# Four order edges, and four products ahead of the bonus sums, in the token mixers of a decoder layer

## The chip, the cores and the metric

The kernel runs on one core of a Trainium2 chip. The metric is the device time of one execution in microseconds. The engines are TensorE (PE in the profile; its weight loads are PEld), VectorE (DVE), ScalarE (ACT), GpSimd (POOL) and SyncE (SP), which here only issues loads. Each engine works through its own list of instructions in the order in which it was written, and semaphores hold an instruction until what it needs is there.

## The reference

One decoder layer on 256 tokens of width 2048, all in float32. The part that matters here is the mixer: one input product `z = rms_norm(x) @ w_in` (2048 by 4384), whose columns go to a causal pooling mixer (1024 columns) and to RWKV-7 time mixing (16 heads of 64). Each RWKV part is shifted in time before use:

```python
def token_shift(z, mu):                      # zr, zk, zv and the gates
    z_prev = pad(z)[:, :-1]
    return z + (z_prev - z) * mu

def step(S, inp):                            # per head, S is 64 x 64
    r_t, w_t, k_t, v_t, a_t, b_t = inp       # a = -kk, b = kk * gate, kk = k normed per head
    sa = einsum('bhij,bhj->bhi', S, a_t)
    S = S * w_t[:, :, None, :] + sa[..., None] * b_t[:, :, None, :] + v_t[..., None] * k_t[:, :, None, :]
    return S, einsum('bhij,bhj->bhi', S, r_t)

y = group_norm(y) + sum(r * k * r_k, -1) * v   # the second term is the "bonus"
x = x + concat(pool_out, y * g) @ w_out
```

A squared-ReLU channel mixer (2048 to 8192 and back), a gated embedding input and a last RMSNorm follow. The change does not touch these.

## The kernel before

Every large product is done as three float32r products: a weight panel `raw` of 128 x 1024 is loaded, ScalarE casts it into the high part `wh` (two casts of 512, L167) and VectorE subtracts to get the low part `wl` (L168, `split_w`). TensorE then does high by high, high by low and low by high. Panels, high parts and low parts have three buffers each. `gemm_toks` is a generator of such products; a product of the input matrix has eight panels, with twelve matmuls of 512 columns for each (L241, L242, L238).

The order on TensorE is written by hand. A queue holds the generators of the input products, in the order zk0, zr0, zv0, zk1, zr1, zp0, zv1, zp1 (the digit is the head group, or the half of the pool columns). `fill(us)` takes about so many microseconds of matmuls from the head of that queue and puts them between the small products of the RWKV part, so that TensorE has work while the other engines prepare the next small product. `finish` takes a generator to its end. On VectorE, ScalarE and GpSimd a scheduler sets the order: it works with its own estimate of times and takes what it holds to be ready, by program order and by the numbers given to `tc.high_priority`. `tc.issue_after(x)` adds an edge: what is issued inside it stands behind `x` in the order.

The RWKV part is done in chunks of 64 tokens, for two groups of eight heads each, called 0 and 1:

- `z_product`: the product's banks are copied with the norm's scale (zk1s, L488), transposed back to columns on TensorE (zkT, L498) and shifted: ScalarE writes `zk_t` (L335), VectorE adds the earlier token (L336).
- `rwkv_k`: squares of the keys (tF, L585), their sums (kkn, L595), the reciprocal norm, and the operands BK and AR of the scores. `rwkv_r` adds the part with zr.
- `inverse`: the inverse of a triangular 32 x 32 block of all heads, as 31 dependent steps on VectorE. Each step is two small operations on the tile X (L724 multiplies, L728 adds); then X is transposed and copied out (L732 to L743). It is a generator too; `beside` and `pace` let it move on a step for each so many microseconds of queue work, and `run` takes it to its end.
- `rwkv_values`: products vt, whose copies go to the tiles UV (L783), and the bonus sums bsum (L523), multiplied by VectorE (L788).
- `rwkv_scores`: for each chunk c a pair of banks of products sc (L669), copied under the mask into SC by VectorE (L676).
- `rwkv_merge`, then `rwkv_core`: chunk by chunk, rym (L821, L834) is copied to R (L818), multiplied to um (L854), copied to UV (L858), multiplied to the state's increment sm (L863), which is copied or added into the state sbd (L872, L874).
- `pool_in` copies the banks of zp0 to a tile zt (L950).

The small products draw on four banks with the tag "rw", which are given out again when their reader is done. zr1's transposes, the bonus sums and the first two pairs of scores of group 1 use the same two of them, one after the other.

The change and the prediction speak of the place between the products zk1 and zv1: group 1 gets its keys and scores, while the inverse of group 0 runs beside them, and then the core of group 0 runs with the inverse of group 1 beside it.

## Time and profile before

| | |
|---|---|
| three runs | 1176.19, 1178.42, 1178.53 us (median 1178.42) |
| profiled execution | 1177.08 us, of which the span is 1175.1 |
| TensorE | 1160.5 us busy, 6407 matmuls |
| VectorE | 877.2 us busy |
| ScalarE | 713.3 us busy |
| granted TensorE clock | 0.998 |
| mixers | from 0 to about 330 us of the span |

The rows of the prediction come from several views of one profiled execution. The page gives the busy time of each engine and the chain of work that ended last. The list of waits gives, for an instruction's line, whom it waited for, the sum, the count and the longest. Rows of the timeline give start, time, engine, line, operation, the tile written and the tiles read (buffer numbers left out), sizes, the count of instructions that were merged, and in brackets the engine's idle time ahead of it and what ended it. The view by windows gives the busy time of each engine inside a stretch. A row's time holds the way through the engine, so the next instruction of an engine often starts before the row's end; how fast an engine goes on is read from the starts.

### The profile page before, as it was taken

Reading aid. Unit: us, or ns where it says so; the run is one execution under the profiler, and the core shown is the slowest. Engines: PE = TensorE matmul, PEld = TensorE weight load, DVE = VectorE, ACT = ScalarE, POOL = GpSimd, SP = SyncE. Lnnn points to the kernel's source line nnn. Section 1 sums busy time; section 2 is a strip of 40 time slices with the busy share of each in tenths; the row PEclk is TensorE's granted clock in tenths of the full one; section 3 lists DMA queues with packets and bytes.
Section 4 is the critical chain, followed back from the end, with each engine's and each line's share of the span. In section 5 each row is a group of like instructions: output and inputs, shape, how many; then the busy total and the mean of one; then the engine's idle time right before and its main releaser. Section 6 shows DMA issues by size and latency. Waiting matters only on the chain.

```text
span 1175.1 us, 17401 instructions
## 1 busy us (share of the span) xinstructions
PE 1160.5 (99%) x6407; PEld 971.5 (83%) x6407; DVE 877.2 (75%) x1194; ACT 713.3 (61%) x1323; POOL 57.2 (5%) x133
## 2 busy tenths in 40 slices
PE   9999999999999999999999999999999999999997
PEld 8788777888888888888888888888888888888886
DVE  8686996964656666766998997676768988897543
ACT  8776858676545565555664664555556665677543
POOL 2100000000000000000110110000000110000000
PEclk9999999999999999999999999999999999999999
DMA  8464443354465555565686787555555886975511
GB/s 293 155 202 145 138 137 120 120 180 153 169 199 172 185 181 197 191 220 181 204 254 222 220 253 223 188 190 191 185 193 171 253 253 220 320 245 190 197 55 72
DMA packets 67253, 224.42 MB, mean 191 GB/s; under 512 B 7712, under 2 KB 8480, under 8 KB 66784
## 3 DMA queue, kind: packets, MB, share of 16 engines
q1 hardware_dynamic: 60240, 207.38, 51.6%
q0 software_dynamic: 6496, 15.21, 5.7%
q8 instruction: 50, 0.82, 0.3%
q10 hardware_dynamic: 432, 0.73, 0.2%
q14 instruction: 35, 0.29, 0.1%
HBM read 221.19 MB, written 2.10 MB: 190 GB/s over the span
## 4 chain that ended last, share of the span: by engine, by line
PE 95%; DVE 2%; ACT 1%; issue 0%; DMA 0%; POOL 0%; SPq 0%; DVEq 0%; POOLq 0%
PE u_w L1112 20%; PE u_w L1117 10%; PE d_b L1270 7%; PE d_b L1269 7%; PE d_b L1271 7%; PE d_w L1270 2%; PE d_w L1269 2%; PE d_w L1271 2%; PE gt_b L241 2%; PE gt_b L242 2%; PE gt_b L238 2%; PE zk_b L241 1%; PE zk_b L242 1%; PE o_b L238 1%; PE o_b L241 1%; PE o_b L242 1%
## 5 line engine op out<-in xcount | busy, mean ns | idle before, releaser
L1112 PE MATMUL u_w<-h,wh_u 128*128 128x512 f32 x1024 | 321.9, 396 | 0.0
L167 ACT ACTIVATE wh_u<-raw_u 128x512 fp32r<-128x512 f32 x256 | 147.6, 624 | 162.5 <-issue 100.9
L168 DVE TENSOR_TENSOR wl_u<-raw_u,wh_u 128x1024 fp32r<-128x1024 f32 x128 | 156.6, 1224 | 105.0 <-ACT wh_u L167 103.5
L1117 PEld LDWEIGHTS u_w<-h,wl_u 128*128 128x128 f32 x1024 | 192.5, 188 | 45.3
L1117 PE MATMUL u_w<-h,wl_u 128*128 128x256 f32 x1024 | 201.2, 278 | 0.0
L1112 PEld LDWEIGHTS u_w<-h,wh_u 128*128 128x128 f32 x1024 | 156.0, 189 | 0.2
L168 DVE TENSOR_TENSOR wl_gt<-raw_gt,wh_gt 128x1024 fp32r<-128x1024 f32 x24 | 29.4, 1224 | 23.3 <-ACT wh_gt L167 23.1
L172 ACT ACTIVATE wad<-ring 128x512 fp32r<-128x512 f32 x29 | 18.2, 628 | 44.2 <-DVE ring L1320 44.2
L167 ACT ACTIVATE wh_gt<-raw_gt 128x512 fp32r<-128x512 f32 x48 | 27.9, 635 | 24.3 <-PE gt_b L242 17.1
L241 PE MATMUL gt_b<-wh_gt,h 128*128 128x512 f32 x96 | 37.5, 390 | 0.0
L242 PE MATMUL gt_b<-wh_gt,h 128*128 128x512 f32 x96 | 37.4, 390 | 0.0
L1322 DVE TENSOR_TENSOR raw_d<-raw_d,ring 128x1024 f32<-128x1024 f32 x29 | 35.5, 1223 | 0.7
L1239 POOL DMA_DIRECT2D ring<-in_w_ffn_down_dram x29 | 16.5, 568 | 355.8 <-DVE wad L173 355.2
L1240 POOL DMA_DIRECT2D ring<-in_w_ffn_down_dram x29 | 25.4, 874 | 110.9 <-DMA ring<-in_w_ffn_down_dram 110.9
L168 DVE TENSOR_TENSOR wl_o<-raw_o,wh_o 128x1024 fp32r<-128x1024 f32 x16 | 19.6, 1222 | 12.9 <-ACT wh_o L167 9.9
L167 ACT ACTIVATE wh_o<-raw_o 128x512 fp32r<-128x512 f32 x32 | 18.4, 623 | 16.3 <-issue 8.5
L167 ACT ACTIVATE wh_zp<-raw_zp 128x512 fp32r<-128x512 f32 x32 | 18.6, 623 | 15.7 <-PE zp_b L242 7.2
L168 DVE TENSOR_TENSOR wl_zk<-raw_zk,wh_zk 128x1024 fp32r<-128x1024 f32 x16 | 19.4, 1220 | 9.1 <-ACT wh_zk L167 9.1
L241 PE MATMUL zv_b<-wh_zv,hTh 128*128 128x512 f32 x64 | 26.0, 406 | 0.0
L238 PE MATMUL gt_b<-wl_gt,h 128*128 128x512 f32 x96 | 25.8, 389 | 0.0
L241 PE MATMUL zp_b<-wh_zp,hTh 128*128 128x512 f32 x64 | 25.7, 401 | 0.0
L168 DVE TENSOR_TENSOR wl_zv<-raw_zv,wh_zv 128x1024 fp32r<-128x1024 f32 x16 | 19.4, 1218 | 8.2 <-ACT wh_zv L167 7.3
(927 smaller groups left out, 3012.4 us busy)
## 6 DMA issues: line engine op xcount, KB each, us to landing
raw_u<-in_w_ffn_up_dram SPq DMA_DIRECT2D x128, 512.0 KB, 4.2
raw_d<-in_w_ffn_down_dram SPq DMA_DIRECT2D x99, 512.0 KB, 4.9
ring<-in_w_ffn_down_dram POOLq DMA_DIRECT2D x58, 256.0 KB, 5.0
raw_gt<-in_w_ple_gate_dram SPq DMA_DIRECT2D x24, 512.0 KB, 4.1
raw_zk<-in_w_in_dram SPq DMA_DIRECT2D x16, 512.0 KB, 3.8
raw_zr<-in_w_in_dram SPq DMA_DIRECT2D x16, 512.0 KB, 3.3
raw_zv<-in_w_in_dram SPq DMA_DIRECT2D x16, 512.0 KB, 3.3
raw_zp<-in_w_in_dram SPq DMA_DIRECT2D x16, 512.0 KB, 3.2
```

The costliest lines, as they stand in the source:

```text
L167: nc.scalar.activation(wh[:, a * 512 : (a + 1) * 512], raw[:, a * 512 : (a + 1) * 512], AF.Copy)
L168: nc.vector.tensor_tensor(wl, raw, wh.bitcast(F32), op=ALU.subtract)
L238: nc.tensor.matmul(banks[tt], ah[:, ts_], halves[a][1], start=False, stop=last)
L241: nc.tensor.matmul(banks[tt], ah[:, ts_], halves[a][0], start=i + a == 0, stop=False)
L242: nc.tensor.matmul(banks[tt], al[:, ts_], halves[a][0], start=False, stop=False)
L1112: nc.tensor.matmul(bank[:, ct, :].rearrange("p (s t) -> p s t", s=2), wh[:, cs[ct]], hl, start=k == 0, stop=False, skip_group_check=True,)
L1117: nc.tensor.matmul(bank[:, ct, 0:T], wl[:, cs[ct]], hl[:, 0, :], start=False, stop=k == 15, skip_group_check=True)
L1240: nc.gpsimd.dma_start(slot(n), w_down[pair, hf * 16 + kp, 0, :, 1, :], accum_op=ALU.add)
L1269: nc.tensor.matmul(banks[n], ah, wh, start=first, stop=False)
L1270: nc.tensor.matmul(banks[n], ah, wl, start=False, stop=False)
L1271: nc.tensor.matmul(banks[n], al, wh, start=False, stop=last)
L1322: nc.vector.tensor_tensor(t43, t43, t2.unsqueeze(1).to_broadcast([128, 2, 512]), op=ALU.subtract)
```

## The change

Nothing that is computed changes, and no instruction is added. Four edges are added, most of them through a table `behind`, and one fill:

- the casts of panel zr1_2 stand behind the second copy zk1s;
- step 17 of the inverse of group 0 stands behind the last key shift of group 1, and the generator waits for that shift to have been written down;
- the casts of panel zv1_2 stand behind the copies R of the first chunk of group 0;
- the copies zt of the first pool product stand behind the first UV copy of the core (`started`); before, they were made when that product ended;
- `rwkv_values` takes 0.90 us of queue work (four low-part matmuls of zp0) between the vt products and the bonus sums for group 0, and the fill ahead of group 1's scores is cut from 8.39 to 7.47 for it.

```diff
--- before.py
+++ after.py
@@ -158,13 +158,14 @@
         nc.sync.dma_start(raw[:, 0:n], src)
         return raw
 
-    def split_w(raw, name):
+    def split_w(raw, name, after=None):
 
         wh = wp.tile([128, 1024], F32R, tag="wh", name=f"wh_{name}")
         wl = wp.tile([128, 1024], F32R, tag="wl", name=f"wl_{name}")
         with tc.high_priority(20000):
             for a in range(2):
-                nc.scalar.activation(wh[:, a * 512 : (a + 1) * 512], raw[:, a * 512 : (a + 1) * 512], AF.Copy)
+                with tc.issue_after(after.ins) if after is not None else ExitStack():
+                    nc.scalar.activation(wh[:, a * 512 : (a + 1) * 512], raw[:, a * 512 : (a + 1) * 512], AF.Copy)
             nc.vector.tensor_tensor(wl, raw, wh.bitcast(F32), op=ALU.subtract)
         return [(t_h, t_l) for t_h, t_l in zip((wh[:, 0:512], wh[:, 512:1024]), (wl[:, 0:512], wl[:, 512:1024]))]
 
@@ -216,6 +217,8 @@
                             yield 0.24
         consume(banks)
 
+    behind = {}
+
     def gemm_toks(src, acts, name, consume, kps=None, hooks=()):
 
         banks = [mm_bank(f"{name}_b{i}") for i in range(2)]
@@ -225,7 +228,7 @@
             if kp in hooks:
                 hooks[kp]()
             raw = load_raw(src[kp].rearrange("p a n -> p (a n)"), 1024, f"{name}_{kp}")
-            halves = split_w(raw, f"{name}_{kp}")
+            halves = split_w(raw, f"{name}_{kp}", behind.get(f"{name}_{kp}"))
             for part in range(2):
                 for a in range(2):
                     k = kp * 2 + a
@@ -333,7 +336,7 @@
 
     def shift_evac(dst, src, mu_ap, omu_ap):
         nc.scalar.activation(dst, src, AF.Copy, scale=omu_ap)
-        nc.vector.scalar_tensor_tensor(
+        return nc.vector.scalar_tensor_tensor(
             dst[:, 1:T], src[:, 0 : T - 1], mu_ap, dst[:, 1:T], op0=ALU.mult, op1=ALU.add
         )
 
@@ -485,7 +488,9 @@
                 zt = rp.tile([128, 2, 512], F32, tag=stage, name=f"{tag}{gi}s")
             with tc.high_priority(30000):
                 for tt in range(2):
-                    nc.scalar.activation(zt[:, tt], banks[tt], AF.Copy, scale=rs1[:, tt : tt + 1])
+                    copied = nc.scalar.activation(zt[:, tt], banks[tt], AF.Copy, scale=rs1[:, tt : tt + 1])
+            if (tag, gi) == ("zk", 1):
+                behind["zr1_2"] = copied
             box.append(zt)
 
         def turn():
@@ -499,7 +504,9 @@
             for p in range(4):
                 c = PARAM_COLS[mu_name] - m0 + 4 * gi + p
                 with tc.high_priority(30000):
-                    shift_evac(dst[:, p, :], banks[p // 2][:, p % 2 * T : (p % 2 + 1) * T], col(mu_name, 4 * gi + p), omu[:, c : c + 1])
+                    shifted = shift_evac(dst[:, p, :], banks[p // 2][:, p % 2 * T : (p % 2 + 1) * T], col(mu_name, 4 * gi + p), omu[:, c : c + 1])
+            if (tag, gi) == ("zk", 1):
+                behind["key"] = shifted
             return dst
 
         gen = queued(gemm_toks(w_in[i + gi], hT, f"{tag}{gi}", consume))
@@ -721,10 +728,13 @@
         for k in range(31):
             n, m = k // 2 + 1, 31 - k
             t_ = X.rearrange("u j t -> u (j t)")[:, 512 : 512 + n * m].rearrange("u (j t) -> u j t", t=m)
-            nc.vector.tensor_tensor(
-                t_, W[:, 0:n, k : k + 1].to_broadcast([128, n, m]),
-                AT[:, k, k + 1 : 32].unsqueeze(1).to_broadcast([128, n, m]), op=ALU.mult,
-            )
+            while gi == 0 and k == 17 and "key" not in behind:
+                yield
+            with tc.issue_after(behind["key"].ins) if gi == 0 and k == 17 else ExitStack():
+                nc.vector.tensor_tensor(
+                    t_, W[:, 0:n, k : k + 1].to_broadcast([128, n, m]),
+                    AT[:, k, k + 1 : 32].unsqueeze(1).to_broadcast([128, n, m]), op=ALU.mult,
+                )
             nc.vector.tensor_tensor(W[:, 0:n, k + 1 : 32], W[:, 0:n, k + 1 : 32], t_, op=ALU.add)
             yield
         T1G = rp.tile([96, 32, 32], F32, tag=tags[0], name=f"T1G{gi}")
@@ -781,6 +791,7 @@
             for i in range(2):
                 with tc.high_priority(30000):
                     nc.scalar.activation(flat3(UV[2 * tt + i])[64:128], b[i * 64 : (i + 1) * 64, :], AF.Copy)
+        fill(0.00 if gi else 0.90)
         bon = st["rk"]
         bf, vf = flat(bon), flat(zv)
         block_sum(
@@ -791,7 +802,7 @@
         )
         st["UV"] = UV
 
-    def rwkv_core(gi, st):
+    def rwkv_core(gi, st, started=None):
         AR, pc, SC, BKt, UV = st["AR"], st["pc"], st["SC"], st["BKt"], st["UV"]
 
         YT = yb(gi, 1)
@@ -815,7 +826,8 @@
             d = flat3(dst).rearrange("s (q r x) -> s q r x", q=2, r=2)
             v = b.rearrange("s (q r x) -> s q r x", q=2, r=2)
             for r in range(2):
-                nc.scalar.activation(d[:, :, r], v[half(2 * r, y), :, r], AF.Copy)
+                copied = nc.scalar.activation(d[:, :, r], v[half(2 * r, y), :, r], AF.Copy)
+            return copied
 
         def direct(b, c, h):
             nc.tensor.matmul(
@@ -837,7 +849,9 @@
                     )
             R = Rs[:, c % 2]
             with tc.high_priority(30000):
-                two_halves(R, b, False)
+                copied = two_halves(R, b, False)
+            if (gi, c) == (0, 0):
+                behind["zv1_2"] = copied
             if 0 < c < 3:
                 for e in range(2):
                     r = slice(e * 64, e * 64 + 64)
@@ -855,7 +869,10 @@
                 if c < 3:
                     direct(b_next, c + 1, h)
             with tc.high_priority(30000):
-                nc.scalar.activation(flat3(UV[c])[0:64], ub[0:64, :], AF.Copy)
+                copied = nc.scalar.activation(flat3(UV[c])[0:64], ub[0:64, :], AF.Copy)
+            if c == 0 and started is not None:
+                with tc.issue_after(copied.ins):
+                    started()
             fill(0.72 if gi else 0.86)
             if c < 3:
                 for h in range(8):
@@ -1007,7 +1024,7 @@
     z_zk1 = z_product(4, "zk", "mu_k", 1)
     z_zr1 = z_product(2, "zr", "mu_r", 1)
     pool = []
-    p_zp0 = queued(gemm_toks(w_in[0], hT, "zp0", lambda banks: pool.append(pool_in(0, banks))))
+    p_zp0 = queued(gemm_toks(w_in[0], hT, "zp0", pool.append))
     z_zv1 = z_product(6, "zv", "mu_v", 1, "zr")
     p_zp1 = queued(gemm_toks(w_in[1], hT, "zp1", lambda banks: pool.append(pool_in(1, banks))))
 
@@ -1034,13 +1051,17 @@
     beside.clear()
     rwkv_values(0, st0, zv0)
     make_bands()
-    fill(8.39)
+    fill(7.47)
     rwkv_scores(1, st1)
     fill(0.00)
     rwkv_merge(0, st0)
     beside += [inverse(1, st1), 0.50, 0.0]
     fill(3.06)
-    core0 = rwkv_core(0, st0)
+
+    def first_pool():
+        pool[0] = pool_in(0, pool[0])
+
+    core0 = rwkv_core(0, st0, first_pool)
     mg0 = a8(0, "mg0", F32R)
     rwkv_out(0, *rwkv_norm1(0, *core0), mg0)
     rwkv_sources(1, st1)
```

On TensorE one thing moves: `bsum` stands behind four `zp_b` matmuls of L238 instead of ahead of them. The lists of GpSimd and of the loads stay as they are. On VectorE and ScalarE the scheduler makes of the edges more than they say. Three places matter.

VectorE, up to the end of the key shifts of group 1 (wl_zr1_* are subtracts, X0 the inverse of group 0, zk_t the key shifts). Before, behind the subtract of panel zr1_1 and the operations of 126 and 130 elements that now follow the shifts:

```order
L168 TENSOR_TENSOR wl_zr1_2_1412<-raw_zr1_2_1409,wh_zr1_2_1411 128x1024
L724 TENSOR_TENSOR X0_1131<-X0_1131,AT0_1130 128x120
L728 TENSOR_TENSOR X0_1131<-X0_1131 128x10x12
L724 TENSOR_TENSOR X0_1131<-X0_1131,AT0_1130 128x121
L336 SCALAR_TENSOR_TENSOR zk_t_1349<-zkT0_1350,par_sb_77,zk_t_1349 128x255
L728 TENSOR_TENSOR X0_1131<-X0_1131 128x11x11
L336 SCALAR_TENSOR_TENSOR zk_t_1349<-zkT1_1351,par_sb_77,zk_t_1349 128x255
L724 TENSOR_TENSOR X0_1131<-X0_1131,AT0_1130 128x110
L728 TENSOR_TENSOR X0_1131<-X0_1131 128x11x10
L336 SCALAR_TENSOR_TENSOR zk_t_1349<-zkT0_1350,par_sb_77,zk_t_1349 128x255
L724 TENSOR_TENSOR X0_1131<-X0_1131,AT0_1130 128x108
L336 SCALAR_TENSOR_TENSOR zk_t_1349<-zkT1_1351,par_sb_77,zk_t_1349 128x255
```

Now:

```order
L169 TENSOR_TENSOR wl_zr1_1_1389<-raw_zr1_1_1386,wh_zr1_1_1388 128x1024
L169 TENSOR_TENSOR wl_zr1_2_1412<-raw_zr1_2_1409,wh_zr1_2_1411 128x1024
L339 SCALAR_TENSOR_TENSOR zk_t_1349<-zkT0_1350,par_sb_77,zk_t_1349 128x255
L339 SCALAR_TENSOR_TENSOR zk_t_1349<-zkT1_1351,par_sb_77,zk_t_1349 128x255
L169 TENSOR_TENSOR wl_zr1_3_1446<-raw_zr1_3_1443,wh_zr1_3_1445 128x1024
L339 SCALAR_TENSOR_TENSOR zk_t_1349<-zkT0_1350,par_sb_77,zk_t_1349 128x255
L339 SCALAR_TENSOR_TENSOR zk_t_1349<-zkT1_1351,par_sb_77,zk_t_1349 128x255
L734 TENSOR_TENSOR X0_1131<-X0_1131,AT0_1130 128x126
L738 TENSOR_TENSOR X0_1131<-X0_1131 128x9x14
L734 TENSOR_TENSOR X0_1131<-X0_1131,AT0_1130 128x130
L738 TENSOR_TENSOR X0_1131<-X0_1131 128x10x13
L734 TENSOR_TENSOR X0_1131<-X0_1131,AT0_1130 128x120
```

The shifts stand ahead of eleven inverse operations that were ahead of the last of them; the subtract wl_zr1_3, which stood behind, comes between them.

VectorE, the end of the inverse of group 0 and the first copies of the scores of group 1 (T1G0 and the STREAM_TRANSPOSE rows finish the inverse; SC1 are the score copies). Before:

```order
L732 STREAM_TRANSPOSE T1G0_1646<-X0_1131 32x16x32
L168 TENSOR_TENSOR wl_zp0_4_1778<-raw_zp0_4_1775,wh_zp0_4_1777 128x1024
L732 STREAM_TRANSPOSE T1G0_1646<-X0_1131 32x16x32
L735 COPY tmp0_1132<-X0_1131 64x16x32 x2
L739 STREAM_TRANSPOSE X0_1131<-tmp0_1132 64x16x32
L168 TENSOR_TENSOR wl_zp0_5_1809<-raw_zp0_5_1806,wh_zp0_5_1808 128x1024
L739 STREAM_TRANSPOSE X0_1131<-tmp0_1132 64x16x32
L676 TENSOR_TENSOR SC1_1759<-sc0_1760,cmask_93 128x2x4x64
L676 TENSOR_TENSOR SC1_1759<-sc1_1761,cmask_93 128x2x4x64
L168 TENSOR_TENSOR wl_zp0_6_1840<-raw_zp0_6_1837,wh_zp0_6_1839 128x1024
L676 TENSOR_TENSOR SC1_1759<-sc0_1791,cmask_93 128x2x4x64
L676 TENSOR_TENSOR SC1_1759<-sc1_1792,cmask_93 128x2x4x64
```

Now:

```order
L734 TENSOR_TENSOR X0_1131<-X0_1131,AT0_1130 128x30
L738 TENSOR_TENSOR X0_1131<-X0_1131 128x15x2
L734 TENSOR_TENSOR X0_1131<-X0_1131,AT0_1130 128x16
L738 TENSOR_TENSOR X0_1131<-X0_1131 128x16
L742 STREAM_TRANSPOSE T1G0_1646<-X0_1131 32x16x32 x2
L745 COPY tmp0_1132<-X0_1131 64x16x32 x2
L169 TENSOR_TENSOR wl_zp0_6_1840<-raw_zp0_6_1837,wh_zp0_6_1839 128x1024
L749 STREAM_TRANSPOSE X0_1131<-tmp0_1132 64x16x32 x2
L683 TENSOR_TENSOR SC1_1759<-sc0_1760,cmask_93 128x2x4x64
L683 TENSOR_TENSOR SC1_1759<-sc1_1761,cmask_93 128x2x4x64
L683 TENSOR_TENSOR SC1_1759<-sc0_1791,cmask_93 128x2x4x64
L683 TENSOR_TENSOR SC1_1759<-sc1_1792,cmask_93 128x2x4x64
```

All of the inverse still stands ahead of the first score copies; the subtract wl_zp0_6, which stood behind them, stands ahead of them too.

ScalarE, from the last merge copies into SC0 on (zt0 the pool copies, R0, UV0_0 and sbd1 the core of group 0, tmp1 the start of the inverse of group 1). Before:

```order
L764 ACTIVATE SC0_950<-qm_1900 32x8x32 x4
L950 ACTIVATE zt0_1942<-zp0_b0_1584,rs_n1_175 128x512
L950 ACTIVATE zt0_1942<-zp0_b1_1585,rs_n1_175 128x512
L167 ACTIVATE wh_zv1_2_2073<-raw_zv1_2_2071 128x512
L818 ACTIVATE R0_1966<-rym_1971 64x2x128 x2
L167 ACTIVATE wh_zv1_2_2073<-raw_zv1_2_2071 128x512
L167 ACTIVATE wh_zv1_3_2149<-raw_zv1_3_2147 128x512 x2
L710 ACTIVATE tmp1_1927<-tmp1_1927 64x1024
L858 ACTIVATE UV0_0_1655<-um_1991 64x512
L872 ACTIVATE sbd1_96<-sm_1992 64x4x64 x2
L818 ACTIVATE ys0_1967<-rym_1971 64x2x128
L719 ACTIVATE tmp1_1927<-SC1_1759 32x1024
```

Now:

```order
L774 ACTIVATE SC0_950<-qm_1900 32x8x32 x4
L717 ACTIVATE tmp1_1927<-tmp1_1927 64x1024
L829 ACTIVATE R0_1963<-rym_1968 64x2x128 x2
L168 ACTIVATE wh_zv1_2_2073<-raw_zv1_2_2071 128x512 x2
L168 ACTIVATE wh_zv1_3_2149<-raw_zv1_3_2147 128x512 x2
L726 ACTIVATE tmp1_1927<-SC1_1759 32x1024
L872 ACTIVATE UV0_0_1655<-um_1988 64x512
L967 ACTIVATE zt0_2008<-zp0_b0_1584,rs_n1_175 128x512
L967 ACTIVATE zt0_2008<-zp0_b1_1585,rs_n1_175 128x512
L889 ACTIVATE sbd1_96<-sm_1989 64x4x64 x2
L829 ACTIVATE ys0_1964<-rym_1968 64x2x128 x2
```

The pool copies go behind UV0_0, the copy inside tmp1 goes ahead of R0, and the second tmp1 copy ahead of UV0_0.

## The prediction

> **What bounds the kernel now.** I read the page first, then the waits of TensorE, then the rows of TensorE, VectorE and ScalarE in order of time around each wait.
>
> ```profile
> span 1175.1 us, 17401 instructions
> PE 1160.5 (99%) x6407; PEld 971.5 (83%) x6407; DVE 877.2 (75%) x1194; ACT 713.3 (61%) x1323; POOL 57.2 (5%) x133
> ...
> PE 95%; DVE 2%; ACT 1%; issue 0%; DMA 0%; POOL 0%; SPq 0%; DVEq 0%; POOLq 0%
> ```
>
> TensorE is the bound, and 95% of the chain that ended last lies on it. A change of order can only win back the time in which TensorE waits. The waits of TensorE between 100 and 262 us are four:
>
> ```profile
> PE bsum L523 <- DVE zr_t L336: 1.0, 1, 1.0
> PE sm L863 <- ACT UV L858: 0.9, 1, 0.9
> PE zkT L498 <- ACT zk1s L488: 0.8, 2, 0.5
> PE um L854 <- ACT R L818: 0.4, 1, 0.4
> ```
>
> These are idle times. A matmul's row is longer than the 0.23 us in which the next one starts, so a little more is hidden; the starts show it (start, time, then the group):
>
> ```profile
> 127.06 0.39 PE L242 MATMUL zr_b<-wh_zr,hTl 128*128 128x512 f32 x1
> 127.98 0.33 PE L498 MATMUL zkT<-ident,zk1s 128*128 128x128 f32 x1 [0.53 <-ACT zk1s L488]
> 128.56 0.98 PE L498 MATMUL zkT<-ident,zk1s 128*128 128x128 f32 x7 [0.25 <-ACT zk1s L488]
> 129.30 0.48 PE L241 MATMUL zr_b<-wh_zr,hTh 128*128 128x512 f32 x1
> ...
> 134.02 2.16 PE L595 MATMUL kkn<-tF_t,jhead 128*32 128x256 f32 x8
> 136.11 0.50 PE L241 MATMUL zr_b<-wh_zr,hTh 128*128 128x512 f32 x1
> ...
> 156.07 1.95 PE L780 MATMUL vt<-cen,zv_t 128*128 128x128 f32 x16
> 159.01 1.96 PE L523 MATMUL bsum<-ybuf,jsum 128*128 128x512 f32 x4 [0.99 <-DVE zr_t L336]
> ...
> 173.03 0.39 PE L238 MATMUL zp_b<-wl_zp,hTh 128*128 128x512 f32 x1
> 173.35 1.26 PE L669 MATMUL sc<-AR,BK 64*128 64x128 f32 x16
> ```
>
> The change works on all of these but the last pair, which I come to below: the second group of scores starts at 173.35, only 0.1 later than the end of the matmul in front of it allows. That row decides my forecast.
>
> **The change part by part: what TensorE wins first.** ScalarE's rows there:
>
> ```profile
> 125.18 2.18 ACT L167 ACTIVATE wh_zr<-raw_zr 128x512 fp32r<-128x512 f32 x4
> 127.26 1.24 ACT L488 ACTIVATE zk1s<-zk_b,rs_n 128x512 f32<-128x512 f32 x2
> ...
> 134.20 1.31 ACT L585 ACTIVATE tF_t<-zk_t,par_sb 128x256 f32<-128x256 f32 x3 [0.23 <-DVE zk_t L336]
> ```
>
> The edge behind the key copies puts two of the four casts (0.52 each) after zk1s, so zk1s runs from 126.2 to 127.5. TensorE comes to the transposes at 127.29, and only the second of them still waits, for some 0.2. I count 1.0 won of the 1.2 between 127.29 and 128.56.
>
> The key shifts then pass eleven operations of the inverse on VectorE (each of its steps is two, L724 and L728). Walked through the new order they end at 132.9 (the last one now starts at 134.26, below). But on ScalarE half a cast (0.52) stands between the second and the third of the four squares tF (0.4 each), so the last square ends near 134.4, where 134.20 + 1.31 = 135.5 is its end now. The norm products kkn, which go one by one behind the squares, therefore end 1.1 earlier. This contains the 1.0; it does not add to it. Another 0.2 goes at the next products, which wait for the split of the reciprocal.
>
> The bonus sums bsum reuse the banks of the zr transposes and wait for VectorE's shifts of them. Four products, 4 x 0.23 = 0.9, now fill that wait, and the shifts come 2 us earlier because fewer inverse operations stand ahead of them. The wait of 159.01 - 157.86 = 1.15 goes (157.86: the sixteenth vt start of 0.11 each after 156.07). TensorE's total lead at this point is 1.1 + 0.2 + 1.15 = 2.4 us.
>
> **Where the lead ends.** The operations that were passed have not gone: they stand behind, on VectorE.
>
> ```profile
> core 0: us, PE busy (x) PEld busy (x) DVE busy (x) ACT busy (x) POOL busy (x), PEclk, DMA share, GB/s
> 129.07:173.40 44.33, 43.19 (x213) 33.52 (x211) 43.37 (x78) 25.94 (x48) 1.86 (x5) 1.00 0.45 151
> ```
>
> Between the first moved operation and the end of the first score copies VectorE is busy 43.37 of 44.33 us. It has no room to catch up in.
>
> ```profile
> 129.07 0.28 DVE L724 TENSOR_TENSOR X<-X,AT 128x126 f32<-128x126 f32 x1
> 129.39 0.29 DVE L728 TENSOR_TENSOR X<-X 128x126 f32<-128x126 f32 x1
> ...
> 132.02 0.29 DVE L724 TENSOR_TENSOR X<-X,AT 128x121 f32<-128x121 f32 x1
> 132.22 0.47 DVE L336 SCALAR_TENSOR_TENSOR zk_t<-zkT,par_sb,zk_t 128x255 f32<-128x255 f32 x1
> ...
> 134.26 0.47 DVE L336 SCALAR_TENSOR_TENSOR zk_t<-zkT,par_sb,zk_t 128x255 f32<-128x255 f32 x1
> ...
> 172.17 1.23 DVE L676 TENSOR_TENSOR SC<-sc,cmask 128x512 f32<-128x512 f32 x2
> 173.34 1.20 DVE L168 TENSOR_TENSOR wl_zp<-raw_zp,wh_zp 128x1024 fp32r<-128x1024 f32 x1
> 174.55 1.29 DVE L676 TENSOR_TENSOR SC<-sc,cmask 128x512 f32<-128x512 f32 x2
> ```
>
> The score copies stand behind the whole inverse of the first head group, before and after. The second group of score products (173.35) uses the two banks that the first copies (172.17 to 173.4) free; it starts as they end. In the new order everything that stood ahead of these copies still does, and one subtract more: wl_zp0_6, which is the row at 173.34 now. So the copies end later by three terms:
>
> - the subtract, 174.55 - 173.34 = 1.2;
> - new waits of VectorE, by my walk 0.4 at wl_zr1_4 (its cast is the one that stands between the squares), 0.3 at the split of the reciprocal (two casts now stand ahead of it), 0.3 at the first zr shift, which VectorE reaches before ScalarE has written it, and 0.2 at wl_zp0_3, whose buffer the four moved products free: 1.2. Of the 0.96 idle now I take half for waits and half for gaps between operations: 0.7 net;
> - an inverse operation right behind another starts 0.32 later (129.07, 129.39), other work starts 0.20 later (132.02, 132.22). Nineteen such pairs stand in the new stretch and sixteen in the old: 3 x 0.12 = 0.4.
>
> That is 2.3: the second scores start at 175.65 instead of 173.35. TensorE arrives there at 173.26 - 2.4 = 170.8 and waits 4.8 us. **The whole lead is lost and 2.3 us more.** Bounds: 0.2 (1.2 less all 0.96 of idle, no new wait) and 3.4 (every new wait, none of the old ones gone). I take the middle, which is where the walk ends.
>
> [...]
>
> **The core's copies and the late adds.**
>
> ```profile
> 190.33 1.27 ACT L950 ACTIVATE zt<-zp_b,rs_n 128x512 f32<-128x512 f32 x2
> 192.01 0.77 ACT L818 ACTIVATE R<-rym 64x256 f32<-64x256 f32 x2
> 194.36 1.06 ACT L710 ACTIVATE tmp<-tmp 64x1024 f32<-64x1024 f32 x1
> 195.45 0.59 ACT L858 ACTIVATE UV<-um 64x512 f32<-64x512 f32 x1
> 198.04 1.05 ACT L719 ACTIVATE tmp<-SC 32x1024 f32<-32x1024 f32 x1
> ...
> 193.33 2.36 DVE L168 TENSOR_TENSOR wl_zv<-raw_zv,wh_zv 128x1024 fp32r<-128x1024 f32 x2 [7.34 <-ACT wh_zv L167]
> 205.51 0.86 DVE L874 TENSOR_TENSOR sbd<-sbd,sm 64x256 f32<-64x256 f32 x2
> ...
> 206.73 0.39 PE L834 MATMUL rym<-sbd,AR 128*128 128x128 f32 x2
> ```
>
> All of this is counted from the end of the scores and moves with it. The panel copies zt (1.2) leave the place ahead of R, and the L710 copy takes it, so R ends 0.65 earlier, which covers most of the um wait. But ahead of UV there would stand 1.07 (L710), 0.65 (R), 4 x 0.52 (casts) and 1.06 (L719, moved up): 4.86 after 190.33, that is 195.2 instead of 195.45. The wait for um has become a longer wait for sm; the gain is 0.25. Bounds: 1.9 won if the casts yield, 0.5 lost if ScalarE comes later.
>
> The second inverse starts earlier (its transposed tile is ready at 191.4, where VectorE sat idle until 193.33), and the scheduler uses that to put nine more inverse operations, 9 x 0.31 = 2.8, ahead of the state add of 205.51. It starts 1.9 earlier and has 2.8 more to do: the add ends at 207.3 and not at 206.4. TensorE wants it at 206.73 - 0.25 = 206.5 and waits 0.8, so 0.55 is lost against now. Bounds 0 and 0.9.
>
> **The sum.** 2.3 - 0.25 + 0.55 = 2.6 us. The profiled execution took 1177.08 (span 1175.1 and 2.0 around it), which makes 1179.7. It lies 1.3 under the median of the three runs, 1178.42, so for a median I add the 2.6 to that: **1181.0 us**. Nothing after 260 us changes its order, and TensorE's own work is the same.
>
> **The rivals.**
>
> *Faster: the lead survives.* If VectorE reached the first score copies by 170.8, TensorE would keep 2.4, and 0.25 in the core: 1178.4 - 2.65 = 1175.8. For it: the four waits are real, and each edit lies on one. Against it: VectorE would have to do in under 42 us what takes 43.4 now, with one subtract more. It decides from the point where VectorE is 5 us sooner through this stretch than I walk. Chance 0.2.
>
> *No change.* VectorE finds room for the subtract in its own 0.96 of idle time, or the inverse's pairs go at 0.20 like single operations (19 x 0.12 = 2.3 less). The second scores then start 0 to 0.2 later than now, the core's 0.25 cancels that, and the late add is left or not: 1178.4 to 1178.9. For it: each new wait is under 0.5 us, and I walked them by hand. Chance 0.27.
>
> *Slower still.* The third scores need a bank that ScalarE frees with the L783 copies, which stand behind the two L743 copies and so behind the end of the inverse. I have them done 1.3 before TensorE comes. If the inverse ends 2 us later than I walk, its lateness passes to this wait as well: 1178.4 + 4.6 = 1183.0. Chance 0.08. The forecast keeps 0.45.
>
> **How the numbers follow.** A measurement of this kernel tells about 0.2%, 2.4 us, from no change. The forecast's 2.6 lies just over that; I give it 0.38 beyond and 0.07 inside. With the last rival, slower has 0.46; faster has 0.19 of its 0.2; the rest, 0.35, is no change. The range reaches from the fast rival, 1175.6, to the slow one, 1183.2; the forecast's own range is 1179 to 1182.5.
>
> **What would show it.** Right: the list of TensorE's waits no longer has bsum or zkT above 0.3, and has a new one, the score products waiting 4 to 5 us for VectorE near 171 to 176; VectorE has no idle time over 0.5 from 129 until then; sm still waits for UV, more than 1 us; a rym wait on the state add near 209. Wrong: no wait of TensorE at the scores, or the first score copies ending before 174. If that wait is under 2 us, the term of VectorE is mis-sized and the kernel is not slower.

## The result and the profile after

The changed kernel takes 1184.18 us (median of six, 1182.72 to 1185.0), the kernel before, beside it, 1177.87 (1176.19 to 1179.46). The ratio is 1.0054, with a 95% interval of 1.0044 to 1.0064: slower by 6.3 us, 5.2 to 7.5. The direction is the forecast's; the size, 2.6, is not. Of all executions behind the numbers below, one is left out: 2342 us in an experiment (e6), which nothing else repeats.

The page's own lines, after:

```profile
span 1183.0 us, 17400 instructions
PE 1163.5 (98%) x6407; PEld 973.6 (82%) x6407; DVE 878.3 (74%) x1194; ACT 713.0 (60%) x1323; POOL 57.3 (5%) x133
...
PE 90%; DVE 6%; ACT 1%; DMA 1%; issue 1%; SPq 0%; DVEq 0%; ACTq 0%
```

VectorE has 6% of the chain where it had 2%. TensorE's list of waits (total, times, longest; the changed kernel's lines stand 3 to 21 lower in the file: the score products are L676 now, the score copies L683, the weight products L241, L244 and L245):

```profile
PE sc L676 <- DVE SC L683: 4.6, 1, 4.6
PE wagT L467 <- ACT wagS L462: 1.9, 1, 1.9
PE sm L880 <- ACT UV L872: 1.4, 1, 1.4
...
PE rym L846 <- DVE sbd L891: 0.7, 1, 0.7
...
PE yt L930 <- DVE ys L924: 0.3, 1, 0.3
```

Three of the four old waits between 100 and 262 us are gone (bsum, zkT, um). One of 4.6 us has come, beside two short ones (rym, yt): the second group of score products waits for VectorE's score copies. VectorE's rows there, with the subtract wl_zp0_6 in front of the first copies, which started at 172.17 before:

```profile
173.55 1.23 DVE L169 TENSOR_TENSOR wl_zp<-raw_zp,wh_zp 128x1024 fp32r<-128x1024 f32 x1
174.70 2.06 DVE L749 STREAM_TRANSPOSE X<-tmp 64x512 f32<-64x512 f32 x2
176.67 1.23 DVE L683 TENSOR_TENSOR SC<-sc,cmask 128x512 f32<-128x512 f32 x2
```

What the prediction had not counted stands right behind that wait. TensorE's rows in order of time:

```profile
172.44 0.39 PE L241 MATMUL zp_b<-wl_zp,hTh 128*128 128x512 f32 x1
177.46 2.64 PE L676 MATMUL sc<-AR,BK 64*128 64x128 f32 x16 [4.62 <-DVE SC L683]
180.03 1.65 PE L241 MATMUL zp_b<-wl_zp,hTh 128*128 128x512 f32 x3
181.47 0.63 PE L244 MATMUL zp_b<-wh_zp,hTh 128*128 128x512 f32 x1
```

The sixteen score products take 2.64 us; before they took 1.26 (the row at 173.35 in the prediction). The next matmuls are slow as well: 0.43 from start to start at 181.47, where it is 0.23 at full speed. The view by stretches says why, in the column behind POOL: PEclk, the share of its clock that TensorE was granted.

```profile
168.46:171.88 3.42, 3.42 (x27) 2.70 (x26) 3.17 (x10) 2.32 (x6) 0.00 (x0) 1.00 0.50 169
171.88:175.29 3.41, 0.95 (x5) 0.45 (x3) 3.35 (x5) 1.15 (x2) 0.00 (x0) 1.00 0.00 0
175.29:178.70 3.41, 1.24 (x8) 1.18 (x10) 2.62 (x4) 1.83 (x2) 0.00 (x0) 0.50 0.46 154
178.70:182.12 3.42, 3.42 (x17) 2.81 (x16) 1.64 (x3) 2.85 (x7) 0.00 (x0) 0.50 0.00 0
182.12:185.53 3.41, 3.41 (x26) 2.62 (x26) 1.26 (x2) 1.71 (x5) 0.00 (x0) 1.00 0.42 151
```

From 175.29 to 182.12 the clock is at half. TensorE works in the last 4.66 us of that (from 177.46) and does half as much: 4.66 / 2 = 2.3 us are lost behind the wait.

**The whole difference between the two profiled executions**, 1184.91 - 1177.08 = 7.8 us, read from the start of the same matmul in both:

| stretch | what | us |
|---|---|---|
| to 60 us | longer wagT wait and a half clock behind it, in a part that the change leaves as it was | +2.39 |
| 125 to 171 | TensorE's lead: less waiting at zkT, kkn, the next products, bsum | -2.98 |
| 172 to 177 | the wait at the second scores | +4.70 |
| 177 to 184 | half clock | +2.34 |
| 186 to 205 | um and sm together | -0.06 |
| 213 | rym, late state add | +1.04 |
| 214 to 245 | yt and around it | +0.55 |
| behind 600 | several small ones | -0.18 |

The first row is no work of the change: such a stretch comes and goes in other programs too (last section). Without it, it is 5.4 us.

### The profile page after: what moved, and what is told of

Same layout as the page of the kernel before. It is cut to its first block, busy times and chain, and to the rows that moved or that the text cites. A ratio compares the mean times of both kernels' runs of the same rounds, so it can differ in the third digit from the quotient of the medians.

```text
span 1183.0 us, 17400 instructions
## 1 busy us (share of the span) xinstructions
PE 1163.5 (98%) x6407; PEld 973.6 (82%) x6407; DVE 878.3 (74%) x1194; ACT 713.0 (60%) x1323; POOL 57.3 (5%) x133
## 4 chain that ended last, share of the span: by engine, by line
PE 90%; DVE 6%; ACT 1%; DMA 1%; issue 1%; SPq 0%; DVEq 0%; ACTq 0%
PE u_w L1133 20%; PE u_w L1138 10%; PE d_b L1291 7%; PE d_b L1292 7%; PE d_b L1290 7%; PE d_w L1290 2%; PE d_w L1291 2%; PE d_w L1292 2%; PE gt_b L244 2%; PE gt_b L245 2%; PE gt_b L241 2%; PE zr_b L244 1%; PE zr_b L241 1%; PE o_b L244 1%; PE o_b L241 1%; PE zr_b L245 1%
## 5 line engine op out<-in xcount | busy, mean ns | idle before, releaser
L244 PE MATMUL gt_b<-wh_gt,h 128*128 128x512 f32 x96 | 37.4, 390 | 0.0
L245 PE MATMUL gt_b<-wh_gt,h 128*128 128x512 f32 x96 | 37.4, 389 | 0.0
L244 PE MATMUL zp_b<-wh_zp,hTh 128*128 128x512 f32 x64 | 26.3, 411 | 0.0
L244 PE MATMUL zk_b<-wh_zk,hTh 128*128 128x512 f32 x64 | 25.9, 405 | 0.3 <-ACT wh_zk L168 0.3
L244 PE MATMUL zv_b<-wh_zv,hTh 128*128 128x512 f32 x64 | 26.0, 406 | 0.0
L241 PE MATMUL gt_b<-wl_gt,h 128*128 128x512 f32 x96 | 25.8, 389 | 0.0
```

The source lines that it names most:

```text
L241: nc.tensor.matmul(banks[tt], ah[:, ts_], halves[a][1], start=False, stop=last)
L244: nc.tensor.matmul(banks[tt], ah[:, ts_], halves[a][0], start=i + a == 0, stop=False)
L245: nc.tensor.matmul(banks[tt], al[:, ts_], halves[a][0], start=False, stop=False)
```

## The experiments

Ratios are to the kernel before, timed beside each run. Microseconds are the ratio's distance from 1 times 1177.5.

**Without the inverse edge.** The `while` and the `issue_after` at step 17 are removed; every other edit stays.

```diff
-            while gi == 0 and k == 17 and "key" not in behind:
-                yield
-            with tc.issue_after(behind["key"].ins) if gi == 0 and k == 17 else ExitStack():
...
```

> The changed kernel without the edge that holds step 17 of the first inverse behind the key shifts; every other edit stays. Theory (the loss is made by VectorE reaching the score copies late, because of the moved inverse operations, and by TensorE's half clock after the long wait): VectorE does before the score copies what it did in the kernel before, so the second group of score products starts within 0.7 us of its old distance from the start of the first zr product of group 1; TensorE, ahead by about 2, waits there 1.5 to 3 us, and its granted clock falls for at most 1 us. Time within 1.5 us of before (1176.5 to 1179.5). Rival (the edges on ScalarE and the moved panel copies make the loss): still 3 us or more over before, 1181 or later.

1.0028 (1.0016 to 1.0039): +3.3 us. The wait at the scores and its half clock are gone as the theory expected (sc 0.4), but the time is the rival's. Rows of its waits:

```profile
PE kkn L602 <- ACT tF_t L592: 2.7, 2, 1.7
PE sm L877 <- ACT UV L869: 2.3, 2, 1.4
...
PE rym L843 <- DVE sbd L888: 0.7, 1, 0.7
...
PE sc L676 <- DVE SC L683: 0.4, 1, 0.4
```

The key shifts come behind ten inverse operations and a subtract (133.58 on VectorE; 132.63 in the changed kernel, whose head ran 2.1 us later), and a second subtract stands between the first two shifts and the last two. The casts that ScalarE does behind zk1s feed these subtracts. So the squares are late and kkn waits 2.7, which neither side expected. That the edge on these casts does it is read from the order of the rows; no run takes that edge out alone. At 162 us the lead over the kernel before is 0.2, counted from 60 us on, where the changed kernel has 3.0. With no lead left, the rest is loss: 1.0 up to the second scores, 1.2 at the late state add, 0.5 around yt, 1.1 behind 246 us, where sm of the second group waits 0.9; 0.6 comes back behind 600 us.

**The inverse edge alone**, on the kernel before.

```diff
+            if (tag, gi) == ("zk", 1):
+                behind["key"] = shifted
...
+            while gi == 0 and k == 17 and "key" not in behind:
+                yield
+            with tc.issue_after(behind["key"].ins) if gi == 0 and k == 17 else ExitStack():
```

> The kernel before with only the edge that holds step 17 of the first inverse behind the key shifts. Theory: the score copies end 1.5 to 2.5 us later than before, TensorE is about 1 to 2 us earlier there and waits 3 to 5 us, and the granted clock then stands at 0.50 for some 4 us: time over before by 3.5 to 6.5 us (1181.5 to 1184.5), most of the loss of the changed kernel. Rival (the other edges): within 1.2 us of before.

1.0044 (1.0032 to 1.0056): +5.2 us, as the theory said. From its list of waits:

```profile
PE sc L673 <- DVE SC L680: 3.6, 2, 3.2
```

and by stretches, with the clock behind the POOL column:

```profile
170.31:173.72 3.41, 1.06 (x5) 0.45 (x3) 3.38 (x5) 1.15 (x2) 0.00 (x0) 1.00 0.10 20
173.72:177.13 3.41, 2.16 (x15) 1.97 (x16) 1.57 (x3) 2.71 (x4) 0.00 (x0) 0.50 0.34 133
177.13:180.55 3.42, 3.42 (x9) 2.65 (x10) 2.05 (x3) 1.97 (x5) 0.00 (x0) 0.50 0.00 0
180.55:183.96 3.41, 3.41 (x27) 2.61 (x26) 1.21 (x2) 2.32 (x6) 0.00 (x0) 1.00 0.47 156
```

One edge is enough for the late copies (the second of them starts 1.6 later than before, counted from 60 us on), the wait and the half clock.

**What a wait costs, made on purpose.** In the kernel before, products are moved from in front of the second scores to behind them, so that TensorE comes 4.7 (e3) or 2.6 us (e4) too early. The edit of e3; e4 has 5.20 in place of 7.29 and leaves the 8.39 as it is:

```diff
-                fill(2.60 if gi else 4.55)
+                fill((0.00, 7.29, 2.60)[c - 1] if gi else 4.55)
...
-    fill(8.39)
+    fill(6.30)
```

> The kernel before with 4.7 us of weight products taken from in front of the second group of score products (2.1 of them from in front of the first) and put behind it, in front of the third; nothing else is edited. TensorE then reaches the second group 4.7 us early and waits about 4.8 us for the copies of the first; from the third group on its order is the old one. Theory (a wait of this length also halves the clock afterwards): over before by 4.7 + 2 to 3, that is 6.5 to 8 us (1184.5 to 1186), with a granted clock of 0.50 in about 4 us behind the wait. Rival (a wait costs its own length): over before by 4.2 to 5.2 us, clock 1.00 right behind the wait.

1.0059 (1.0047 to 1.0071): +6.9 us. In its list of waits:

```profile
PE sc L669 <- DVE SC L676: 4.3, 1, 4.3
```

Counted from start to start the wait is 4.53, and TensorE is 6.2 later behind the scores.

> The same with 2.6 us of products moved from in front of the second group to in front of the third: TensorE waits about 2.7 us. Theory, if the clock falls only after a wait longer than this: over before by 2.3 to 3 us, clock 1.00 behind the wait. If the clock falls after any wait in proportion: over before by 4 us or more. Rival (the products only have to be done somewhere, and the wait is hidden): within 1 us of before.

1.0035 (1.0023 to 1.0048): +4.1 us, for a wait of 2.3 in the list, 2.56 from start to start:

```profile
PE sc L669 <- DVE SC L676: 2.3, 1, 2.3
```

The stretches of the smaller one:

```profile
170.04:173.45 3.41, 1.10 (x12) 0.91 (x14) 2.74 (x4) 1.71 (x2) 0.00 (x0) 1.00 0.41 154
173.45:176.86 3.41, 3.41 (x14) 2.70 (x13) 2.11 (x3) 3.34 (x9) 0.00 (x0) 0.50 0.00 0
176.86:180.27 3.41, 3.41 (x16) 2.78 (x16) 1.18 (x2) 1.95 (x5) 0.00 (x0) 1.00 0.47 154
```

Both waits bring one stretch of 3.41 us at half clock, 1.7 us of loss, whatever their length. The wait of 2.56 costs about 1.7 times its length. That the clock needs a longer wait, as one expectation had it, is wrong.

**The wait filled with work that is worth nothing**: products of the identity with zeros, added into the panel's open bank. e5 has ten of them, e9 five.

```diff
+            if gi and c == 1:
+                for _ in range(10):
+                    nc.tensor.matmul(behind["zp0"][0], ident, sbd[0].rearrange("p a t -> p (a t)"), start=False, stop=False)
```

> The changed kernel with ten products of the identity with a tile of zeros (128x512 fp32, some 0.45 us each) in front of the second group of scores of head group 1, added into the open bank of the panel: TensorE has work in the 4.8 us in which it waits, and nothing ends earlier by it. Theory (behind the wait the loss is the half clock, because TensorE was idle): the second scores start where they start in the changed kernel, the granted clock behind them is 1.00, and the time is 2 to 2.4 us below the changed kernel: over before by 3 to 4.5 us instead of 6.3. Rival (the rows behind the wait are slow by the new order of the other engines, or by the score copies): clock 0.50 as before, over before by 5.5 to 7.5 us.

1.0064 (1.0052 to 1.0076): +7.5 us, the rival's number, but not for its reason. A product took 0.87 us and not 0.45, so ten ran 3.9 us past the wait. Behind it, and from 50 us on to the last microseconds, the clock was 1.00. Five fit:

> e5 with five products of zeros instead of ten. Ten took 8.7 us (0.87 each, not 0.45), 3.9 longer than the wait; five take 4.35 and fit into it. Theory (half clock after an idle TensorE): the second scores start within 0.6 us of their place in the changed kernel, the granted clock behind them is 1.00, no stretch of 0.50 between 50 us and 1100 us, and the time is 2 to 2.5 us below the changed kernel: over before by 3 to 4.6 us. Rival (the loss behind the wait has another cause): over before by 5.5 us or more.

1.0034 (1.0022 to 1.0047): +4.0 us against 6.3. TensorE's rows (the trace has two matmuls for each of the five products):

```profile
170.78 4.45 PE L675 MATMUL zp_b<-sbd,ident 128*128 128x512 f32 x10
175.66 1.73 PE L679 MATMUL sc<-AR,BK 64*128 64x128 f32 x16 [0.42 <-DVE SC L686]
```

and the stretch around them:

```profile
169.00:186.00 17.00, 16.44 (x111) 11.34 (x111) 12.39 (x16) 9.29 (x19) 0.00 (x0) 1.00 0.27 94
```

The second scores start no sooner, 4.88 us after TensorE has got there; only the idling is gone. With it go the half clock and 2.3 us: the two intervals (2.6 to 5.5 and 5.2 to 7.5) still overlap a little, but 2.3 is what the table has for the half clock, and from 60 us on this profile is 2.4 shorter than the changed kernel's. So the loss behind the wait is the half clock, and its cause is that TensorE had nothing to do.

**The wait filled with products of the queue.**

```diff
-                fill(2.60 if gi else 4.55)
+                fill((7.20 if c == 1 else 2.60) if gi else 4.55)
```

> The changed kernel with 4.6 us more of weight products in front of the second group of scores (7.2 instead of 2.6); the products come from the same queue, so all later ones stand 4.6 us earlier in it. Theory: the wait of 4.8 us becomes work (below 0.5 us is left), no half clock follows, and what is taken from the queue is missing at its end only: 7 us below the changed kernel, that is from 2 us under to 0.7 us over before. Rival (the products that stand ahead of later waits are what covers them): the waits of the core grow by 2 us or more in all, and the time stays 2 us or more over before.

1.0047 (1.0034 to 1.0061): +5.5 us. That is the rival's side: the products that went are missing later. At the second scores 1.3 us of waiting are left and the half clock is gone. But between gm and qm, the two steps of `rwkv_merge`, the changed kernel has twenty products for the second group; here the queue runs dry after four:

```profile
261.20 1.21 PE L241 MATMUL zp_b<-wl_zp,hTh 128*128 128x512 f32 x4
263.79 0.32 PE L767 MATMUL qm<-SC,T1G 32*64 32x64 f32 x2 [1.38 <-ACT T1G L774]
```

and a little later, by stretches:

```profile
266.11:269.52 3.41, 3.41 (x16) 3.07 (x15) 0.00 (x0) 2.77 (x7) 0.00 (x0) 0.50 0.53 209
```

TensorE waits for qm, and behind that wait the clock is at half again.

**Five subtracts to GpSimd**, in the changed kernel and in the one before, to give VectorE room.

```diff
-            nc.vector.tensor_tensor(wl, raw, wh.bitcast(F32), op=ALU.subtract)
+            (nc.gpsimd if name in ('zp0_1', 'zp0_2', 'zp0_4', 'zp0_5', 'zp0_6') else nc.vector).tensor_tensor(wl, raw, wh.bitcast(F32), op=ALU.subtract)
```

> The changed kernel with the five subtracts wl_zp0_1, 2, 4, 5 and 6 (1.2 us each on VectorE, in front of the first score copies) done by GpSimd. Theory (VectorE's work in front of the score copies is what ends TensorE's lead): the first score copies end 5 to 6 us earlier than in the changed kernel, the wait at the second scores is below 0.7 us, the lead of 3 us survives there, and with the 1.4 us that the core loses the time is 0.5 to 2.5 us under before. Rival (the lead would be lost at another place anyway, such as the third scores, or GpSimd is too slow for these subtracts): same as before or over it.

> The kernel before with the same five subtracts on GpSimd, no other edit. Theory: TensorE waits in the kernel before for ScalarE's key copies and behind the key shifts, not for lack of VectorE's time in the panel; only the 1.2 us in front of the bonus sums may go. So 0 to 1.2 us under before, and e7 is 0.5 us or more below this one: the edits of the change pay once VectorE has room. Rival (the subtracts alone are the gain, the edits do nothing): this run is as fast as e7 or faster.

1.0042 (1.0029 to 1.0055) and 1.0075 (1.0063 to 1.0087): both lose. A row of GpSimd of the second:

```profile
151.11 7.70 POOL L168 TENSOR_TENSOR wl_zp<-raw_zp,wh_zp 128x1024 fp32r<-128x1024 f32 x2 [0.46 <-ACT wh_zp L167]
```

VectorE's rows beside it:

```profile
154.10 2.39 DVE L638 TENSOR_SCALAR AR<-tB_t 128x16 f32<-128x16 f32 x1
...
156.64 2.22 DVE L724 TENSOR_TENSOR X<-X,AT 128x30 f32<-128x30 f32 x1
```

and from its list of waits:

```profile
PE bsum L523 <- DVE zr_t L336: 7.0, 1, 7.0
```

While GpSimd subtracts, single VectorE operations on 16 or 30 elements last 2.2 to 2.4 us; the second of these lasts 0.19 in the changed kernel. The scheduler also put the inverse's steps into the place of the subtracts, in front of the zr shifts, and bsum waits 7.0 us (3.6 in e7). TensorE's lead was spent before it came to the scores, so these two say nothing on the theory.

**The panel copies put back** (`core0 = rwkv_core(0, st0)`, zt copied as the panel ends).

> The changed kernel with the panel copies zt put back to where they stood (they no longer wait for the first UV copy); all else as in the changed kernel. Theory: this edit lets the copy in front of the second inverse go first on ScalarE and so puts six to nine inverse operations in front of the state add of step 1; without it the rym wait of 0.87 and the yt wait of 0.43 go or fall below 0.3 each, the wait at the second scores and the half clock stay: 0.8 to 1.5 us below the changed kernel, over before by 4.5 to 5.7 us. Rival (the second inverse is early for another reason): rym still waits 0.7 or more, no difference.

1.0042 (1.0029 to 1.0055): +4.9 us. The interval overlaps the changed kernel's, so the profile has to tell:

```profile
PE um L868 <- ACT R L829: 1.1, 1, 1.1
PE yt L930 <- DVE ys L924: 0.3, 1, 0.3
...
PE rym L846 <- DVE sbd L891: 0.2, 1, 0.2
```

rym falls from 0.7 to 0.2, so it is this edge that puts the state add late. The wait at yt stays, against the expectation. um waits 1.1 in place of sm's 1.4: on ScalarE the edge moves a wait from um to sm. From the same place at 60 us this profile is 1.1 us shorter.

**The score copies first.** The end of the first inverse goes behind the score copies of the second group, UV0_1 and ys exchange buffers, and the queue work in front of the second, third and fourth scores is 4.1, 2.3 and 2.6 us. e11 is the changed kernel with that and without the zt edge; e12 the kernel before with that order and its own products.

```diff
+            with tc.issue_after(behind["c1"].ins) if gi == 0 else ExitStack():
                 nc.vector.tensor_copy(tmp[0:64, i::2, :], W[i * 64 : i * 64 + 64])
...
-        uvs = [rp.tile([128, 2, 8, 64], F32, tag=f"q{i}", name=f"UV{gi}_{i}") for i in range(2)]
+        uvs = [rp.tile([128, 2, 8, 64], F32, tag=("q0", "q3")[i], name=f"UV{gi}_{i}") for i in range(2)]
...
-        yss = rp.tile([128, 2, 8, 64], F32, tag="q3", name=f"ys{gi}")
+        yss = rp.tile([128, 2, 8, 64], F32, tag="q1", name=f"ys{gi}")
```

> The changed kernel without the move of zt, and with the end of the first inverse (two copies, two transposes on VectorE) put behind the score copies of the second group, UV0_1 and ys with their buffers exchanged so that the bank of the third scores doesn't wait for the inverse, and the products in front of the groups 4.1, 2.3, 2.6 instead of 2.6, 2.6, 2.6. Theory (the lead of 3 us is real and is only lost where the first score copies end): no wait over 1.2 us at any score group, no half clock there, and the time is under before by 0.5 to 3 us. Rival (what passes the scores early waits for the end of the inverse at the merge or in the core instead): waits of 2 us or more at gm, qm, rym or um, same as before or over it.

> The kernel before with the same order (end of the first inverse behind the score copies of the second group, the buffers exchanged, the products as they were) and none of the edits of the change. Theory: TensorE waits for nothing there in the kernel before, so nothing is to be won: within 1 us of before, and e11 is 1.5 us or more faster than this one, which is what the edits of the change are worth once VectorE lets them. Rival (the order alone is the gain): under before by as much as e11.

0.9992 (0.9983 to 1.0001) and 0.9997 (0.9989 to 1.0006). With the same edits on TensorE's waits, 6 us of loss have become nothing: the changed kernel loses by where its score copies stand. (1.5 us more of queue work in front of the second scores, 4.1 in place of 2.6, is part of that; against a wait of 4.6 it can't be all. The first copies start 4.1 us sooner than in the changed kernel, counted from 60 us on.) Neither is measurably faster than before, and that e11 beats e12 is not shown. In e11's profile no score group waits, and at the last product ahead of the second scores TensorE leads the kernel before by 3.1 us, counted from 60 us on. At the start of the up-projection 0.4 is left. Its waits:

```profile
PE um L875 <- ACT R L836: 1.8, 2, 1.4
...
PE sm L887 <- ACT UV L879: 0.5, 1, 0.5
PE qm L774 <- DVE SC L683: 0.5, 1, 0.5
```

**ScalarE's order around R.** e13 is e11 with the zt edge. e14 also holds the 64x1024 copy of the second inverse behind the first R copy.

```diff
+        while gi and "zv1_2" not in behind:
+            yield
+        with tc.issue_after(behind["zv1_2"].ins) if gi else ExitStack():
             nc.scalar.activation(tmp[64:128], tmp[0:64], AF.Copy)
```

> e11 with the panel copies zt behind the first UV copy, as in the change. In e11 the second half of zt (0.69) and the copy in front of the second inverse (1.05) stand ahead of the R copies, and TensorE waits 1.54 for um. Theory: zt leaves that place and um waits 0.2 to 0.9; five casts now stand ahead of UV, so sm waits 0.7 to 1.6 instead, and the state add is late again by up to 1: within 0.8 us of e11, either way. Rival (the edit gains what ScalarE's copies cost): 1.2 us or more under e11.

> e13 with the 64x1024 copy in front of the second inverse (1.05 on ScalarE) held behind the first R copy too, by the same kind of edge. Theory (what is left of the lead is lost to ScalarE's order around R and UV, and to the second inverse's operations in front of the state add): um waits below 0.3, sm below 1.0, rym below 0.3; 1 to 2.5 us under e11, that is 1.5 to 3.5 us under before. Rival (the second inverse then ends too late): a wait of 1 us or more at gm or qm of the second group near 255 to 262, no gain over e11.

1.0003 (0.9994 to 1.0012) and 0.9997 (0.9989 to 1.0006). The waits go in part as expected: in e13 the first um wait goes and sm waits 1.1, but a later um waits 1.4 and the state add is not late; in e14 um waits 0.4 and sm 0.9 in all. The gain that e14's theory forecast, 1.5 to 3.5 us, did not come. In e14's profile 1.5 us of the lead of 3.1 are left at the up-projection (0.6 in e13). In the times nothing of it shows. No version here is measurably faster than the kernel before.

## Why the prediction was wrong in size

The step that failed is in "Where the lead ends": "waits 4.8 us. **The whole lead is lost and 2.3 us more.**" It priced the wait at its own length. The wait is there, at its place (4.62 idle, 4.78 from start to start), but it also halves TensorE's clock behind it: 2.3 us that the sum had at nothing. e9 takes it away, e3 and e4 make it in the kernel before. The profile of before could not show it, since its longest wait in this part is 1.0 us (bsum) and its clock is 1.00 from 8 to 1165 us. The traces after it do: a clock of 0.50 came behind 4.62 us of idle time in the changed kernel, and behind 2.3 us in e4.

Point by point:

- The four waits and the lead. Right in place; 3.0 us, not 2.4. zkT gave 1.0 and bsum 1.2 as said, but kkn added 0.5 to zkT's 1.0, where the prediction had 0.1, and the next products gave 0.3, not 0.2.
- VectorE late at the second scores. Right, and a little less: 1.7 net instead of 2.3. The subtract wl_zp0_6 and the whole inverse do stand ahead of the copies. e2 shows that the inverse edge alone does it (1.6). The upper bound of 3.4 does not come out of its terms (1.2 + 1.2 + 0.4 = 2.8); 1.7 lies below both. The sign that VectorE has no idle time over 0.5 until then came too: the longest is 0.3.
- "um has become a longer wait for sm; the gain is 0.25". The mechanism is right (e10, e13), the gain 0.1.
- The late state add: 1.0 instead of 0.55. Its cause is the zt edge (e10); that it works through the copy of the second inverse, which goes first on ScalarE, is read from the order and was not tested here by itself.
- yt: 0.5 was left out. On VectorE the last reduction of the normalization (L921) now stands behind the transposes that end the second inverse; before, it stood ahead of them. e1 has the wait without the inverse edge and e10 without the zt edge, so it needs neither of them; which edit makes it is open.
- The sum: 5.4 in the profile from 60 us on, 6.3 in the times. 2.3 of the 2.8 missing in the profile are the half clock.
- The rivals. *Faster* named the right point, VectorE 5 us sooner at the score copies; e11 makes 4.1 of that by order, the lead is there, and the core eats most of it. *No change*: VectorE found no room for the subtract, and operations of the inverse start 0.32 apart after the change as well (138.75, 139.07). *Slower still* didn't happen: the third scores wait for nothing in the changed kernel.

## What to carry to other kernels

A wait of TensorE of 2.56 (e4), 4.53 (e3) or 4.78 us (the changed kernel) cost here its length plus the half clock behind it, 1.7, 1.7 and 2.3 us; in e6 half clock came behind one of 1.3 us too (last section). Four waits of 1 us may therefore be cheaper than one of 4; no run here tried it. Where an edge puts work behind something urgent, look for the next thing that the delayed work stands in front of: here the score copies, 40 us later on an engine with 1 us of room. And an edge is judged with the ones that it leans on: the other edits without the inverse edge cost 3 us, the inverse edge without the rest 5.

## What the hardware showed beside this

**In these traces the clock went by fixed stretches.** The half-clock stretches behind the waits at the scores last 3.41 us (e3, e4) or 6.83 (the changed kernel, e2): one or two times 3.41. In the changed kernel half clock starts at 38.76, 175.29 and 1178.81, which are 40 and 294 times 3.413 apart, so one grid runs through its whole trace. Cut along it from 8 to 1165 us, that trace has two stretches at full clock in which TensorE is busy for less than 2 of the 3.41 us (1.49 from 35.35, 0.95 from 171.88), and half clock follows these two and no other. In the kernel before the least busy stretch has 2.43, and the clock stays at 1.00. In e2, e3 and e4 the stretches with 1.06, 0.48 and 1.10 us of work are followed by half clock. A slow stretch was followed by a fast one where it was full of work (3.42 from 178.70), and by another slow one where it was not (1.24 from 175.29; 2.16 in e2). In between, busy time alone does not decide: full clock came behind 2.02 (the changed kernel, from 199.19) and 1.71 (e10), half clock behind 2.35 (e6). At the same place of e10 and e6:

```profile
36.37:39.78 3.41, 1.71 (x11) 1.49 (x12) 1.61 (x7) 2.63 (x7) 2.87 (x12) 1.00 0.44 160
39.78:43.20 3.42, 3.42 (x17) 2.81 (x16) 3.35 (x10) 2.78 (x5) 0.77 (x2) 1.00 0.12 32
...
34.00:37.41 3.41, 2.35 (x15) 1.83 (x13) 1.39 (x2) 2.14 (x6) 1.27 (x5) 1.00 0.62 217
37.41:40.82 3.41, 3.17 (x11) 2.68 (x12) 2.30 (x9) 2.24 (x4) 2.93 (x11) 0.50 0.28 109
```

What decides there is open; in e4 2.3 us of idle time within one stretch were enough.

**It may also be what makes the times of one kernel spread.** In the profiles of the changed kernel and of e6 such a stretch falls near 38 us, in a part that is the same in all programs, behind a wagT wait of 1.9 and 1.3 us; e10 has 1.9 without it. In the changed kernel's profile:

```profile
35.35:38.76 3.41, 1.49 (x12) 1.14 (x12) 1.70 (x5) 2.19 (x5) 2.44 (x9) 1.00 0.73 245
38.76:42.17 3.41, 3.41 (x12) 2.66 (x10) 2.87 (x9) 2.17 (x3) 1.80 (x7) 0.50 0.06 19
42.17:45.58 3.41, 3.41 (x17) 2.80 (x16) 2.10 (x6) 1.51 (x3) 0.00 (x0) 1.00 0.47 154
```

Of 66 executions of the kernel before, those with a mean granted clock of 0.998 have a median of 1176.9 us, with 0.997 it is 1178.0, with 0.996 1178.8. One stretch at half takes some 0.0015 off the mean (3.41 / 2 of 1175 us), so this fits, but only profiles show where an execution lost its clock. A difference of 1 or 2 us between two single executions may be nothing else.

**GpSimd beside VectorE.** A 128x1024 subtract took GpSimd 2.4 us at its shortest (2.37 in e7, 2.39 in e8; 1.2 on VectorE) and 3.5 and 3.9 each in the pairs of 7.07 (e7, from 149.38) and 7.70 us (e8, from 151.11), beside which VectorE worked on 128x1024 operands. Beside the second pair the two VectorE operations in the rows above took 2.39 and 2.22 us, where the kernel before has 0.17 and 0.19; the one between them kept its time (0.20 at 156.41).
